# A hybrid decoder layer on one core: the first super-block loaded once, transposed, its sums of squares taken as fp32 products with a tile of ones

## The chip, the cores and the metric

The kernel runs on one core of a Trainium2 chip. The core has five engines with a queue of instructions each: TensorE (PE in the profile, its weight loads PEld), VectorE (DVE), ScalarE (ACT), GpSimd (POOL) and SyncE (SP), which here only starts transfers (DMA). Each queue runs in its own order; an instruction waits for what it needs from other queues, and everything behind it on its queue waits with it. SBUF is the memory on the chip, with 128 partitions; TensorE writes its results to PSUM.

The metric is the time of one execution on the device in microseconds, as the median of several runs. Before the change three runs took 2046.22, 2046.26 and 2054.05 us.

## The reference, cut to what matters

One layer for 2048 prompt tokens and 64 sample tokens of width 1024, in fp32. Each token is normalised by the root of its mean square, then multiplied by a wide matrix whose columns feed an attention branch, a convolution branch and a spatial gating branch; these are gated, projected and added to the input.

```python
def _rmsnorm(x, w):
    xf = x.astype(jnp.float32)
    r = lax.rsqrt(jnp.mean(xf * xf, axis=-1, keepdims=True) + EPS)
    return (xf * r).astype(x.dtype) * w
...
    xn = _rmsnorm(x, p["norm_w"])
    h = jnp.einsum("btd,de->bte", xn, p["w_in"])
    q, k, v, z_a, gate_b, gate_c, h_b, z_b, u, v_c, z_c, g = _split_cols(h)
...
    m = gates[:, :, 0] * a + gates[:, :, 1] * b + gates[:, :, 2] * c
    return x + jnp.einsum("btd,de->bte", m, p["w_o"])
```

The change concerns only how the first 512 tokens get their normalised `xn`.

## The kernel before

The tokens are worked off in four super-blocks: three of 512 prompt tokens and a last one of 512 prompt and 64 sample tokens. Within a super-block come the phases in turn: keys and values (`kv_phase`), queries (`q_phase`, a product over all token tiles that the profile calls wideS, widepv and ps_mm at lines 312 to 314, and this text the wide product), attention between the products of the convolution and chunk phases, the gates, and the output projection.

Products are made in three passes of a reduced format (fp32r): each fp32 operand is split into a high part (`split`, a copy by ScalarE, line 169) and a low part (a subtraction by VectorE, line 170), and TensorE adds high times high, high times low and low times high. So the normalised input is stored as `xh` and `xl`, with the 1024 features in 8 k tiles of 128 partitions and the tokens along the free dimension. Weights arrive as `raw` (line 119) in 512 KB pieces, three buffers ahead, and are split into `wh` and `wl`.

Later super-blocks are normalised while TensorE works on the one before (`xrstd`, `xsplit`). The first one has nothing ahead of it: `first_block` handles it in four tiles of 128 tokens. Each tile is loaded twice: `xnat` with tokens in the partitions, for the sum of squares (ScalarE's square with its accumulator, line 265), and `xin` transposed, with features in the partitions. `rstd` makes the reciprocal root on GpSimd in two instructions (lines 165 and 166). A transpose on TensorE (line 268) spreads the 128 values over all partitions, ScalarE copies them to `xrbuf` (line 271), and then, for each of the 8 k tiles, VectorE scales `xin` by the norm weight and that value (line 273) and `split` stores the two parts.

Piece 0 of `first_block` is issued before `kv_phase`. Pieces 1 to 3 are issued from inside it: `later(0.25, ...)` queues piece i + 1 so that it runs at the first `tick` of tile i, which `natural` makes after its fourth k tile. The 24 products of a tile (lines 287 to 289, 256 columns each) are thus cut in two by what piece i + 1 puts on TensorE.

TensorE's and SyncE's queues run in the order in which the code issues. The order on ScalarE, VectorE and GpSimd is set by the framework's scheduler when the kernel is built.

Of the kernel before, what the change touches and what calls it, by code (L numbers as in the profile page):

```python
# [10 lines left out]
F32 = mybir.dt.float32  # L11
F32R = mybir.dt.float32r
AF = mybir.ActivationFunctionType
ALU = mybir.AluOpType
AX = mybir.AxisListType

P = 128
D = 1024
# [6 lines left out]
KT = D // P  # L25
SLOPES = [2.0 ** -(h + 1) for h in range(8)]
TMAX = 576
# [21 lines left out]
def trunk_kernel(ctx: ExitStack, tc: tile.TileContext, A, O):  # L49
    nc = tc.nc  # L50
    consts = ctx.enter_context(tc.tile_pool(name="consts", bufs=1))
    res = ctx.enter_context(tc.tile_pool(name="res", bufs=1))
# [9 lines left out]
    def ps_tp():  # L62
        return psum.tile([P, 512], F32, tag="tp", name="ps_tp", bufs=2)
# [51 lines left out]
    def load_to(j):  # L115
        while len(loaded) < min(j, len(units)):
            src = units[len(loaded)][2]
            raw = raws.tile([P, WE], F32, tag="raw", name="raw")
            nc.sync.dma_start(raw[:, : src.shape[1]], src)
            loaded.append(raw)  # L120

    def split_to(j):
        while len(ready) < min(j, len(units)):
            i = len(ready)
            load_to(i + 1)
            n = units[i][2].shape[1]
            wh = wts.tile([P, WE], F32R, tag="wh", name="wh")
            wl = wts.tile([P, WE], F32R, tag="wl", name="wl")
            split(wh[:, :n], wl[:, :n], loaded[i][:, :n])
            loaded[i] = None  # L130
            ready.append((wh, wl))
            load_to(i + 1 + ahead["loads"])
# [11 lines left out]
    def const(name):  # L144
        src = A[name]
        t = consts.tile(list(src.shape), F32, name="c_" + name)
        nc.sync.dma_start(t, src)
        return t

    mhalf = consts.tile([P, 8], F32, name="mhalf")  # L150
    nc.gpsimd.memset(mhalf, -0.5)


    xh = res.tile([P, KT, TMAX], F32R, name="xh")
    xl = res.tile([P, KT, TMAX], F32R, name="xl")
# [1 line left out]
    vst = res.tile([P, 5 * 256 + 128], F32R, name="vst")  # L157
    hist = consts.tile([P, 4, 2], F32, name="hist")

    consts.tile([P, 48], F32, name="pad")  # L160
    nc.vector.memset(hist, 0.0)

    def rstd(out, ssq, n, width):

        nc.gpsimd.tensor_scalar(out, ssq, 1.0 / width, EPS, ALU.mult, ALU.add)
        nc.gpsimd.tensor_tensor(out, out, mhalf[: out.shape[0], :n], ALU.pow)  # L166

    def split(hi, lo, src):
        nc.scalar.copy(hi, src)  # L169
        nc.vector.tensor_tensor(lo, src, hi.bitcast(F32), ALU.subtract)  # L170
# [78 lines left out]
    def first_block():  # L249

        xin = res.tile([P, 8 * TMAX], F32, tag="mh", name="xin")
        xnat = res.tile([P, 8 * TMAX], F32, tag="ml", name="xnat")
        r = small.tile([P, 8], F32, tag="xr", name="xr")
        rbuf = res.tile([P, 4 * TMAX], F32, tag="za", name="xrbuf")
        view = lambda t, i: t[:, i * D:(i + 1) * D].rearrange("p (k t) -> p k t", k=KT)

        def load(i, natural):
            if natural:
                nc.sync.dma_start(xnat[:, i * D:(i + 1) * D], A["xn"][i * P:(i + 1) * P])
            else:  # L260
                nc.sync.dma_start(view(xin, i), A["xt"][:, :, i * P:(i + 1) * P].rearrange("k p t -> p k t"))

        def piece(i):
            sq, x = xnat[:, i * D:(i + 1) * D], view(xin, i)
            nc.scalar.activation(sq, sq, AF.Square, accum_out=r[:, i:i + 1])
            rstd(r[:, i:i + 1], r[:, i:i + 1], 1, D)
            ps = ps_tp()
            nc.tensor.transpose(ps[:, 0:P], r[:, i:i + 1].broadcast_to([P, P]), ident)
            ts = slice(i * P, (i + 1) * P)
            rb = rbuf[:, ts]  # L270
            nc.scalar.copy(rb, ps[:, 0:P])
            for k in range(KT):
                nc.vector.scalar_tensor_tensor(x[:, k], x[:, k], nw[:, k:k + 1], rb, ALU.mult, ALU.mult)
                split(xh[:, k, ts], xl[:, k, ts], x[:, k])
            if i == 3:
                ahead.update(loads=RAWS, splits=AHEAD)

        return load, piece
# [477 lines left out]
    def out_phase(sb, m):  # L756
# [12 lines left out]
        flush()  # L769

    load, prepare = first_block()
    load(0, True)
    nw = const("nw")
    ident = const("ident")
    load_to(1)
    load(0, False)
    load_to(2)
    split_to(1)
    prepare(0)
    split_to(2)  # L780
    for i in range(1, 4):
        load(i, True)
        load(i, False)
    load_to(2 + RAWS)
    knw2 = const("knw2")
    qnw2 = const("qnw2")
# [174 lines left out]
```

## Time and profile before

| | us |
|---|---|
| median of the three runs | 2046.26 |
| the profiled execution | 2048.72 |
| its span, first to last instruction | 2047.0 |
| TensorE busy in it | 2016.7 (99%) |
| VectorE busy | 1050.9 (51%) |
| ScalarE busy | 845.8 (41%) |
| GpSimd busy | 83.5 (4%) |

The busy shares are means over the whole span. A shift in the first super-block's preparation shows in the first of the page's 40 slices only (0.6 of it busy on TensorE, 0.9 or more in all others), so the views to use are those of the first 40 us: which engine waits for which, and the instructions in order of time. A row of the timeline has the start in us, the duration in us, engine, line, operation, tile written and tiles read, shape, count, and in brackets the engine's idle time before it with what ended it. A row of a group has, behind the bar, the busy time in us and the mean duration in ns, and then the idle time before.

### The profile page before, as it was taken

How to read it: one execution, taken by the hardware profiler on the slowest of the kernel's cores; microseconds unless marked ns; L12 is line 12 of the kernel's file. 1: busy time of each engine (PE TensorE's matmuls, PEld its weight loads, DVE VectorE, ACT ScalarE, POOL GpSimd, SP SyncE). 2: the span in 40 equal slices, each digit the busy share in tenths (PEclk: the TensorE clock that was granted, in tenths of full speed). 3: DMA queues.
4: the chain of work that ended last, by engine and by line, in shares of the span. 5: the costliest groups of instructions: out<-in, count | busy, mean ns of one | idle time of the engine just before them, and what ended most of it. 6: DMA issues, size and time to landing. Idle time of an engine off the chain costs nothing.

```text
span 2047.0 us, 27359 instructions
## 1 busy us (share of the span) xinstructions
PE 2016.7 (99%) x10887; PEld 1757.1 (86%) x10887; DVE 1050.9 (51%) x1818; ACT 845.8 (41%) x1462; POOL 83.5 (4%) x134
## 2 busy tenths in 40 slices
PE   6999999999999999999999999999999999999999
PEld 5788888888888888888888888888879999999999
DVE  5686263445588353335478535335537842533332
ACT  4675233332476333333267433333247641322320
POOL 2200000000200000000200000000110000000000
PEclk9999999999999999999999999999999998999999
DMA  6222233336222223336322223334522332222233
GB/s 206 82 83 83 84 101 123 114 119 210 84 82 83 88 78 126 111 93 201 119 83 81 84 82 109 118 108 136 173 83 59 64 114 57 65 85 86 78 104 108
DMA packets 85695, 212.25 MB, mean 104 GB/s; under 512 B 18224, under 2 KB 23344, under 8 KB 85552
## 3 DMA queue, kind: packets, MB, share of 16 engines
q1 hardware_dynamic: 85536, 209.53, 33.2%
q8 instruction: 85, 1.39, 0.3%
q10 hardware_dynamic: 32, 0.98, 0.1%
q14 instruction: 42, 0.34, 0.1%
HBM read 201.46 MB, written 10.00 MB: 103 GB/s over the span
## 4 chain that ended last, share of the span: by engine, by line
PE 93%; DVE 3%; ACT 2%; POOL 1%; issue 0%; DMA 0%; SPq 0%; ACTq 0%; DVEq 0%; POOLq 0%
PE ps_mm L179 26%; PE ps_mm L178 26%; PE ps_mm L180 26%; PE ps_tp L488 1%; PE wideS L313 1%; PE wideS L314 1%; PE wideS L312 1%; POOL qr L166 1%; PE ps_mm L312 1%; PE ps_mm L314 1%; PE ps_mm L313 1%; PE sp L464 1%; PE ps_mm L289 1%; PE ps_mm L287 1%; PE ps_mm L288 1%; PE pv L496 1%
## 5 line engine op out<-in xcount | busy, mean ns | idle before, releaser
L178 PE MATMUL ps_mm<-xh,wh 128*128 128x512 f32 (+1 forms) x2080 | 743.3, 357 | 5.0 <-DVE qn L409 4.5
L180 PE MATMUL ps_mm<-xh,wl 128*128 128x512 f32 (+1 forms) x2080 | 734.4, 353 | 0.0
L179 PE MATMUL ps_mm<-xl,wh 128*128 128x512 f32 (+1 forms) x2080 | 734.3, 353 | 0.0
L170 DVE TENSOR_TENSOR wl<-raw,wh 128x1024 fp32r<-128x1024 f32 x376 | 408.0, 1085 | 576.5 <-ACT wh L169 573.8
L169 ACT CAST wh<-raw 128x1024 fp32r<-128x1024 f32 x376 | 353.5, 941 | 772.1 <-PE ps_mm L179 535.4
L178 PEld LDWEIGHTS ps_mm<-xh,wh 128*128 128x128 f32 x2080 | 393.2, 189 | 51.9 <-issue 4.7
L180 PEld LDWEIGHTS ps_mm<-xh,wl 128*128 128x128 f32 x2080 | 392.6, 189 | 49.6
L179 PEld LDWEIGHTS ps_mm<-xl,wh 128*128 128x128 f32 x2080 | 393.4, 189 | 45.7
L179 PE MATMUL ps_mm<-ml,wh 128*128 128x512 f32 (+1 forms) x320 | 112.5, 351 | 0.3 <-DVE ml L170 0.3
L180 PE MATMUL ps_mm<-mh,wl 128*128 128x512 f32 (+1 forms) x320 | 112.4, 351 | 0.0
L178 PE MATMUL ps_mm<-mh,wh 128*128 128x512 f32 (+1 forms) x320 | 112.4, 351 | 0.0
L744 DVE TENSOR_TENSOR t<-ps_mm,t 128x512 f32<-128x512 f32 (+1 forms) x120 | 71.6, 597 | 73.7 <-PE ps_mm L180 73.7
L728 ACT ACTIVATE t<-ps_mm,c_bg 128x512 f32<-128x512 f32 (+1 forms) x120 | 73.0, 609 | 69.5 <-PE ps_mm L180 69.5
L450 ACT ACTIVATE rbuf<-ps_tp,c_qnw 64x256 fp32r<-64x256 f32 x128 | 60.0, 468 | 39.4 <-DVE rbuf L451 33.4
L179 PEld LDWEIGHTS ps_mm<-ml,wh 128*128 128x128 f32 x320 | 60.0, 188 | 8.0 <-DVE ml L170 0.6
L180 PEld LDWEIGHTS ps_mm<-mh,wl 128*128 128x128 f32 x320 | 60.1, 188 | 7.5
L178 PEld LDWEIGHTS ps_mm<-mh,wh 128*128 128x128 f32 x320 | 60.1, 188 | 7.4
L474 ACT ACTIVATE sbuf<-sbuf,nm 128x256 f32<-128x256 f32 (+1 forms) x128 | 62.8, 492 | 7.1 <-DVE nm L471 6.8
L767 DVE TENSOR_TENSOR xt<-ps_mm,xt 128x512 f32<-128x512 f32 (+1 forms) x40 | 23.9, 597 | 75.1 <-PE ps_mm L180 46.2
L179 PE MATMUL ps_mm<-br2l,wh 128*128 128x512 f32 (+1 forms) x160 | 56.5, 353 | 0.4 <-DVE br2l L170 0.2
L180 PE MATMUL ps_mm<-br2h,wl 128*128 128x512 f32 (+1 forms) x160 | 56.3, 352 | 0.0
L179 PE MATMUL ps_mm<-br1l,wh 128*128 128x512 f32 (+1 forms) x160 | 56.2, 352 | 0.0
(212 smaller groups left out, 2703.3 us busy)
## 6 DMA issues: line engine op xcount, KB each, us to landing
raw<-in_wt SPq DMA_DIRECT2D x208, 512.0 KB
raw<-in_wout SPq DMA_DIRECT2D x96, 256.0 KB
raw<-in_wn SPq DMA_DIRECT2D x40, 512.0 KB
raw<-in_wo SPq DMA_DIRECT2D x32, 512.0 KB
xbuf<-in_xn SPq DMA_DIRECT2D x12, 512.0 KB
xt<-in_xt SPq DMA_DIRECT2D x24, 256.0 KB
out_yt<-xt SPq DMA_DIRECT2D x24, 256.0 KB
xbuf<-in_xt SPq DMA_DIRECT2D x16, 256.0 KB
```

The costliest lines, as they stand in the source:

```text
L169: nc.scalar.copy(hi, src)
L170: nc.vector.tensor_tensor(lo, src, hi.bitcast(F32), ALU.subtract)
L178: nc.tensor.matmul(o, wh[:, ws], rh(k, c0, c1), start=k == 0, stop=False)
L179: nc.tensor.matmul(o, wh[:, ws], rl(k, c0, c1), start=False, stop=False)
L180: nc.tensor.matmul(o, wl[:, ws], rh(k, c0, c1), start=False, stop=k == kts - 1)
L312: nc.tensor.matmul(o, xh[:, k, ts], wh[:, ws], start=k == 0, stop=False)
L313: nc.tensor.matmul(o, xh[:, k, ts], wl[:, ws], start=False, stop=False)
L314: nc.tensor.matmul(o, xl[:, k, ts], wh[:, ws], start=False, stop=k == KT - 1)
L450: nc.scalar.activation(hh[half, :, e], src, AF.Copy, scale=qnw2[es])
L474: nc.scalar.activation(s[:, h, k0:], s[:, h, k0:], AF.Exp, bias=nm[:, h:h + 1], accum_out=den[:, h:h + 1])
L728: nc.scalar.activation(t[:, c0:c1], pg[:, : c1 - c0], AF.Sigmoid, bias=bg[:, 8 * b + d:8 * b + d + 1])
L744: nc.vector.tensor_tensor(t[:, c0:c1], pa[:, : c1 - c0], t[:, c0:c1], ALU.mult)
```

## The change

In the first super-block, `xnat` and its four loads are gone. ScalarE squares the transposed tile `xin` into `sqs`, without its accumulator. TensorE adds the squares over the features: eight fp32 products per token tile, the squared k tile as the weights and two columns of ones as the moving operand, into two columns of a PSUM tile. VectorE copies one of the columns to `r`, GpSimd makes the reciprocal root as before, and the transpose goes to the same PSUM tile. The scaling stays one instruction per k tile; the split is made for four k tiles in one instruction on each of the two engines, 128x512 elements where it was 128x128. The loads are issued in another order: the transposed tile 0 first, tile 1 between the first two weight pieces, then tiles 2 and 3.

```diff
+    ones = consts.tile([P, 2], F32, name="ones")
+    nc.gpsimd.memset(ones, 1.0)
...
-    consts.tile([P, 48], F32, name="pad")
+    consts.tile([P, 40], F32, name="pad")
...
-        xnat = res.tile([P, 8 * TMAX], F32, tag="ml", name="xnat")
+        sqs = res.tile([P, 8 * TMAX], F32, tag="ml", name="sqs")
...
-        def load(i, natural):
-            if natural:
-                nc.sync.dma_start(xnat[:, i * D:(i + 1) * D], A["xn"][i * P:(i + 1) * P])
-            else:
-                nc.sync.dma_start(view(xin, i), A["xt"][:, :, i * P:(i + 1) * P].rearrange("k p t -> p k t"))
+        def load(i):
+            nc.sync.dma_start(view(xin, i), A["xt"][:, :, i * P:(i + 1) * P].rearrange("k p t -> p k t"))
 
         def piece(i):
-            sq, x = xnat[:, i * D:(i + 1) * D], view(xin, i)
-            nc.scalar.activation(sq, sq, AF.Square, accum_out=r[:, i:i + 1])
+            x, sq = view(xin, i), view(sqs, i)
+            nc.scalar.activation(sqs[:, i * D:(i + 1) * D], xin[:, i * D:(i + 1) * D], AF.Square)
+
+            ps = ps_tp()
+            for k in range(KT):
+                nc.tensor.matmul(ps[:, P:P + 2], sq[:, k], ones, start=k == 0, stop=k == KT - 1)
+            nc.vector.tensor_copy(r[:, i:i + 1], ps[:, P:P + 1])
             rstd(r[:, i:i + 1], r[:, i:i + 1], 1, D)
-            ps = ps_tp()
             nc.tensor.transpose(ps[:, 0:P], r[:, i:i + 1].broadcast_to([P, P]), ident)
...
-            for k in range(KT):
-                nc.vector.scalar_tensor_tensor(x[:, k], x[:, k], nw[:, k:k + 1], rb, ALU.mult, ALU.mult)
-                split(xh[:, k, ts], xl[:, k, ts], x[:, k])
+            for k0 in range(0, KT, 4):
+                ks = slice(k0, k0 + 4)
+                for k in range(k0, k0 + 4):
+                    nc.vector.scalar_tensor_tensor(x[:, k], x[:, k], nw[:, k:k + 1], rb, ALU.mult, ALU.mult)
+                split(xh[:, ks, ts], xl[:, ks, ts], x[:, ks])
...
-    load(0, True)
+    load(0)
...
-    load(0, False)
+    load(1)
...
-    for i in range(1, 4):
-        load(i, True)
-        load(i, False)
+    load(2)
+    load(3)
```

How the queues change is read from the order of the built kernels; a row is a line, an operation, the tile written, the tiles read and the shape, and in brackets what it waits for. The order after the first super-block's keys and values is the same on every engine.

On TensorE, before, around the first tile's fourth k tile (lines 287 to 289 are its three products, line 268 the transpose of the second tile's values):

```order
L287 MATMUL ps_mm<-wh,xh 128x256 [waits Activation_49]
L288 MATMUL ps_mm<-wl,xh 128x256
L289 MATMUL ps_mm<-wh,xl 128x256 [waits DVE_49]
L268 MATMUL ps_tp<-c_ident,xr 128x128 [waits Pool_49]
L287 MATMUL ps_mm<-wh,xh 128x256 [waits Activation_49]
L288 MATMUL ps_mm<-wl,xh 128x256 [waits DVE_49]
```

The same place now (the products are lines 292 to 294, the ones' products line 268, the transpose line 271):

```order
L292 MATMUL ps_mm<-wh,xh 128x256
L293 MATMUL ps_mm<-wl,xh 128x256
L294 MATMUL ps_mm<-wh,xl 128x256
L268 MATMUL ps_tp<-ones,sqs 128x2 x8
L271 MATMUL ps_tp<-c_ident,xr 128x128 [waits DVE_49,Pool_49]
L292 MATMUL ps_mm<-wh,xh 128x256 [waits Activation_49]
```

Eight products stand ahead of the transpose, and the transpose waits for GpSimd and VectorE, which need these products' sum.

On VectorE, before, from the second weight split (line 170 with `wl`) into the second tile's scalings (line 273) and subtractions (line 170 with `xl`):

```order
L170 TENSOR_TENSOR wl<-raw,wh 128x1024 [waits DMAHW5_49]
L170 TENSOR_TENSOR xl<-xin,xh 128x128 [waits Activation_49]
L273 SCALAR_TENSOR_TENSOR xin<-xin,c_nw,xrbuf 128x128 [waits DMAHW7_49,Activation_49]
L273 SCALAR_TENSOR_TENSOR xin<-xin,c_nw,xrbuf 128x128 x2
L170 TENSOR_TENSOR xl<-xin,xh 128x128 [waits Activation_49] x2
```

VectorE now, from the copy of the first tile's sum (line 269) into the second tile (the subtraction is line 172, the scaling line 278):

```order
L269 COPY xr<-ps_tp 128x1 [waits PE_49]
L172 TENSOR_TENSOR wl<-raw,wh 128x1024 [waits DMAHW3_49,Activation_49]
L278 SCALAR_TENSOR_TENSOR xin<-xin,c_nw,xrbuf 128x128 [waits DMAHW1_49,DMAHW0_49,Activation_49]
L278 SCALAR_TENSOR_TENSOR xin<-xin,c_nw,xrbuf 128x128 x7
L172 TENSOR_TENSOR xl<-xin,xh 128x4x128 [waits Activation_49]
L172 TENSOR_TENSOR wl<-raw,wh 128x1024 [waits DMAHW5_49]
L172 TENSOR_TENSOR xl<-xin,xh 128x4x128 [waits Activation_49]
L269 COPY xr<-ps_tp 128x1 [waits PE_49]
L278 SCALAR_TENSOR_TENSOR xin<-xin,c_nw,xrbuf 128x128 [waits DMAHW4_49,Activation_49]
L278 SCALAR_TENSOR_TENSOR xin<-xin,c_nw,xrbuf 128x128 x6
L172 TENSOR_TENSOR xl<-xin,xh 128x4x128 [waits Activation_49]
L278 SCALAR_TENSOR_TENSOR xin<-xin,c_nw,xrbuf 128x128
```

Where scalings and subtractions alternated, seven or eight scalings now stand in a row, with one subtraction for four of them; the copy of a tile's sum stands behind the second subtraction of the tile before it.

On ScalarE, the first rows before (line 265 the square, 271 the copy of the transposed values) and now (264 and 274):

```order
L265 ACTIVATE xnat,xr<-xnat 128x1024 [waits DMAHW0_49]
L169 CAST wh<-raw 128x1024 [waits DMAHW3_49]
L271 COPY xrbuf<-ps_tp 128x128 [waits PE_49]
L169 CAST xh<-xin 128x128 [waits DMAHW4_49,DVE_49]
L169 CAST xh<-xin 128x128 [waits DVE_49]
```

```order
L264 ACTIVATE sqs<-xin 128x1024 [waits DMAHW0_49]
L171 CAST wh<-raw 128x1024 [waits DMAHW3_49]
L264 ACTIVATE sqs<-xin 128x1024 [waits DMAHW4_49]
L274 COPY xrbuf<-ps_tp 128x128 [waits PE_49]
L171 CAST wh<-raw 128x1024 [waits DMAHW5_49]
L171 CAST xh<-xin 128x4x128 [waits DVE_49]
```

The square of the second tile now stands between the first weight cast and the first copy, and waits for that tile's load.

## The prediction

> **What bounds the kernel now.** I looked at the windows of the engines first, cut at 35.01 us, then at TensorE's waits up to 36 us, then at the timeline around that cut. Columns of the windows: stretch, length, then busy time and count of PE, PEld, DVE, ACT, POOL, the granted clock, DMA share, GB/s.
>
> ```profile
> 0.00:35.01 35.01, 18.93 (x105) 16.44 (x105) 21.49 (x79) 20.68 (x59) 9.02 (x22) 1.00 0.65 217
> 35.01:2047.00 2011.99, 1997.77 (x10782) 1740.68 (x10782) 1029.45 (x1740) 825.11 (x1403) 74.45 (x112) 0.99 0.33 102
> ...
> PE ps_tp L268 <- POOL xr L166: 8.2, 2, 6.3
> PE ps_mm L287 <- ACT xh L169: 5.7, 5, 4.3
> PE wideS L313 <- DVE wl L170: 1.3, 1, 1.3
> PE ps_mm L289 <- DVE xl L170: 0.9, 2, 0.7
> ...
> 33.74 1.22 DVE L170 TENSOR_TENSOR wl<-raw,wh 128x1024 fp32r<-128x1024 f32 x1
> 35.01 0.50 PE L313 MATMUL wideS<-wl,xh 128*128 128x512 f32 x1 [1.26 <-DVE wl L170]
> ```
>
> From 35.01 us on TensorE is busy 1997.77 of 2011.99 us: that stretch is TensorE's own work and the edit leaves it alone. Before 35.01 it stands still for 16.1 us (35.01 - 18.93), in the four waits listed (8.2 + 5.7 + 1.3 + 0.9). The last of them ends with the weight split at 33.74. So the question is one only: **when does the unbroken wide product begin in the changed kernel, instead of at 35.01 us?** Every microsecond there goes to the end one for one.
>
> **The change, part by part.** The sums of squares leave ScalarE's accumulator for TensorE: per 128-token tile, a square without accumulation, eight fp32 products with the ones, a one-column copy by VectorE, then POOL's two operations, the transpose, ScalarE's copy and the scaling. On TensorE's queue the products and the transpose of tile i+1 stand between the fourth and fifth k tile of tile i. So in every tile TensorE itself now runs the start of a chain whose end it waits for, with all its later products queued behind that transpose. Before, the squares of tiles 2 and 3 were done early, so only two transposes waited.
>
> The chain's links, from rows of before:
>
> ```profile
> 4.23 1.06 ACT L265 ACTIVATE xnat<-xnat 128x1024 f32<-128x1024 f32 x1 [2.15 <-DMA xnat<-in_xn]
> 5.19 0.19 ACT L265 ACTIVATION_READ_ACCUMULATOR xnat<-xnat 128x1 f32 x1
> 5.46 0.19 POOL L165 TENSOR_SCALAR xr<-xr 128x1 f32<-128x1 f32 x1 [4.33 <-ACT xnat L265]
> 6.35 0.47 PE L268 MATMUL ps_tp<-c_ident,xr 128*128 128x128 f32 x1 [6.35 <-POOL xr L166]
> ...
> 16.10 0.48 PE L268 MATMUL ps_tp<-c_ident,xr 128*128 128x128 f32 x1 [1.88 <-POOL xr L166]
> 16.91 0.88 DVE L273 SCALAR_TENSOR_TENSOR xin<-xin,c_nw,xrbuf 128x128 f32<-128x128 f32 x3 [1.56 <-ACT xrbuf L271]
> 18.58 1.13 DVE L273 SCALAR_TENSOR_TENSOR xin<-xin,c_nw,xrbuf 128x128 f32<-128x128 f32 x4
> ...
> L273 DVE SCALAR_TENSOR_TENSOR xin<-xin,c_nw,xrbuf 128x128 f32<-128x128 f32 x32 | 9.5, 345 | 2.5 <-ACT xrbuf L271 2.5
> L170 DVE TENSOR_TENSOR xl<-xbuf,xh 128x512 fp32r<-128x512 f32 x16 | 10.8, 686 | 2.7 <-ACT xh L169 2.7
> L170 DVE TENSOR_TENSOR xl<-xin,xh 128x128 fp32r<-128x128 f32 x32 | 7.5, 284 | 0.0
> 19.63 1.09 DVE L170 TENSOR_TENSOR xl<-xin,xh 128x128 fp32r<-128x128 f32 x5
> L471 DVE TENSOR_TENSOR nm<-nm,nsinkb 128x4 f32<-128x4 f32 x32 | 4.9, 154 | 0.1
> ```
>
> POOL's pair, from ScalarE's end (5.19 + 0.19) to the transpose at 6.35: 0.97 us. Transpose to scaling, 16.10 to 16.91: 0.81. Scalings start every 0.26 ((1.13 - 0.345) / 3): seven take 1.86, eight 2.1. One lo subtraction of four k tiles: 0.69. The copy isn't in the trace; the nearest row is a 128x4 operation of 0.154, and with the end of the last product before it I take 0.4 (bounds 0.15 and 0.9, should a queued subtraction stand ahead).
>
> The products aren't in the trace in this shape either. Nearest are the fp32 products of the sample group:
>
> ```profile
> L671 PE MATMUL ps_tp<-wsd,vn 64*128 64x64 f32 x8 | 1.1, 278 | 0.0
> 1781.57 1.10 PE L671 MATMUL ps_tp<-wsd,vn 64*128 64x64 f32 x8
> 1668.46 0.44 PE L552 MATMUL sps<-sbuf 64*32 64x128 f32 x8
> 20.43 0.41 PE L288 MATMUL ps_mm<-wl,xh 128*128 128x256 f32 x1
> 20.64 0.41 PE L289 MATMUL ps_mm<-wh,xl 128*128 128x256 f32 x1
> 21.01 0.28 PE L288 MATMUL ps_mm<-wl,xh 128*128 128x256 f32 x1
> 21.12 0.28 PE L289 MATMUL ps_mm<-wh,xl 128*128 128x256 f32 x1
> ```
>
> Line 671 is four calls and eight records: two records for each fp32 product, one every 0.118 us ((1.10 - 0.27) / 7), with 128 weight columns as here. Eight products are then 16 records, 1.9 us; the low bound is line 552's 0.025 a record ((0.44 - 0.27) / 7, with 32 weight columns), 0.4 us a tile. I take 0.118, since the weights have the same width. The last four rows show a second thing: up to 20.64 us a 256-column product starts every 0.21 us, from 21.01 on every 0.11 to 0.12, though the granted clock reads 1.00 throughout. TensorE starts at half pace and reached the full one after working unbroken since 16.10. At half pace I double the records: 3.8 us a tile.
>
> What is removed: four loads of xn (2.1 MB), the accumulator reads, and 24 casts and 24 subtractions on ScalarE and VectorE. VectorE gains 32 x 0.20 - 8 x 0.6 - 4 x 0.15 = 1.0 us (0.20 is the start to start of the x5 row; 0.6 is 0.69 less the same 0.08 overlap). The loads hide nothing that TensorE waits for after 10 us; the first one is now in 512-byte pieces, and I take 4.7 us for it where xn was there at 4.23. A later landing moves the first step by as much, and no other.
>
> ```profile
> 14.45 0.96 POOL L165 TENSOR_SCALAR xr<-xr 128x1 f32<-128x1 f32 x1 [8.15 <-ACT xnat L265]
> 13.94 1.22 DVE L170 TENSOR_TENSOR wl<-raw,wh 128x1024 fp32r<-128x1024 f32 x1
> 22.95 0.19 POOL L165 TENSOR_SCALAR xr<-xr 128x1 f32<-128x1 f32 x1 [0.75 <-ACT xnat L265]
> ```
>
> POOL's first operation took 0.96 us at 14.45 instead of the 0.19 at 22.95, beside a weight split on VectorE. In the new order of VectorE a weight split stands right behind the copy of tile 2 and behind that of tile 0: I add 0.8 and 0.4. [...]
>
> What else VectorE has to do in a cycle, beside the weight split and the second lo half:
>
> ```profile
> L323 DVE TENSOR_REDUCE ks<-sq 128x2 f32<-128x128 f32 x4 | 1.1, 281 | 0.0
> L365 DVE TENSOR_TENSOR kd<-ps_mm,kr 128x256 f32<-128x256 f32 x3 | 1.3, 423 | 1.8 <-POOL kr L166 1.8
> L393 DVE TENSOR_TENSOR vst<-ps_mm,vst 128x128 fp32r<-128x128 f32 x3 | 0.9, 284 | 0.0
> L356 DVE SCALAR_TENSOR_TENSOR kst<-ps_tp,c_knw,kst 64x256 fp32r<-64x256 f32 x2 | 1.0, 491 | 0.0
> 10.42 0.87 DVE L273 SCALAR_TENSOR_TENSOR xin<-xin,c_nw,xrbuf 128x128 f32<-128x128 f32 x3
> ```
>
> Weight split, lo half, ks, kd and vst are 1.22 + 0.69 + 0.28 + 0.42 + 0.28 = 2.9 us; they fit beside the products and records of a cycle (1.2 + 1.9).
>
> **The sum.** Tile 0: landing 4.7, square 1.05, records 3.8, copy 0.4, POOL 0.97 + 0.4, 0.81, eight scalings 2.1, subtraction 0.69: 15.0 us. One cycle from a tile's first lo half to the next one's: ten products, 16 records, then 0.4 + 0.97 + 0.81 + 1.86 + 0.69 = 4.73. Cycle 1, half pace at first: 2.1 + 2.9 (between 1.9 and 3.8) + 4.7: 24.7. Cycle 2: 1.2 + 1.9 + 4.7 + 0.8: 33.3. Cycle 3: 7.8: 41.1. Tail: the other half of tile 3 comes 1.5 later (0.26 + 0.49 + 0.28 + 0.69, less what overlaps), its products take 1.3, two transposes and the first wide one 0.5: **44.4 us, where 35.01 was: +9.4**.
>
> The profiled execution is 2048.72 us (span 2047.0 and 1.7 around it), 2.5 above the median of the three runs; its sum becomes 2058.1. Against the median, 2046.26 + 9.4 = 2055.7.
>
> **Rivals.** *Cheap records*, 0.025 each: cycles 2 and 3 lose 1.5 each, cycle 1 2.3, tile 0 only 0.8, as ScalarE's copy then waits behind the square of tile 1 (its load has the place in the queue that tile 0's xin had, which was in use at 10.42). +3.3: 2049.6. Against it: the 128-column row. *Half pace to the end of the stage*, if small products don't raise the clock: +0.9 in cycle 1, 2.8 in each of cycles 2 and 3, 1.0 in the tail, about 2 at the start of the wide product: 9.5 more, 2065.2. For it: the pauses; against it: 4.8 us of work sufficed before. [...] *VectorE sets the pace*, and the chain hides beside its other work: only its 1.0 us of gain shows, 2045.3, no slower. It decides where products, records, copy, POOL and transpose-to-scaling (1.2 + 1.9 + 0.4 + 0.97 + 0.81 = 5.3) fall below the 2.9 us that VectorE has to do meanwhile. Even free records leave 3.4, so it is unlikely.
>
> **Chances.** Forecast (2052.5 to 2059) 0.63, cheap records 0.13, half pace 0.12, four loads 0.05, VectorE's pace 0.07. The range 2049.5 to 2065 leaves out the last and half of the half pace. A measurement can tell about 0.5% (10.2 us) from no change; 2056.5 is that bound, inside the forecast's spread: two fifths of it and the two slow rivals make 0.42 slower. Faster by 10 us would need the wide product at 25 us: 0.02. Within: 0.56.
>
> **What would show it.** Right: the wide product starts near 44 us; four transposes wait for POOL, about 1.4 us each; line 268 has 64 records about 0.12 apart once the pace is full; the lo subtractions are 8 of 0.69; after that the groups are as before. Wrong: other record counts or spacing; a half pace past 25 us; TensorE waiting for VectorE's subtraction behind a weight split rather than for POOL; or the wide product before 38 us.

## The result, and the profile after

The changed kernel took 2065.95 us (median of four runs, 2064.32 to 2068.27), the kernel before 2047.92 us (2046.22 to 2054.05): a ratio of 1.0083, with a 95% interval of 1.0058 to 1.0108. It is slower by 0.8%, 18.0 us of the medians, and the interval excludes 1. The profiled executions are 2064.32 and 2048.72 us, 15.6 apart. The forecast was +9.4, and the time lies 0.95 us above the top of its range. That range was counted from 2046.26, the median of three runs; the kernel before has 2047.92 here, 1.66 us more. The outcome that the prediction held likeliest, a change within its bound of 10.2 us (0.56), did not come; slower, at 0.42, did.

The windows of the changed kernel, cut where the second wide product begins (columns as in the prediction), and TensorE's waits up to 60 us:

```profile
0.00:49.57 49.57, 33.95 (x169) 32.05 (x170) 22.40 (x61) 17.98 (x31) 10.55 (x23) 0.83 0.43 132
49.57:2062.60 2013.03, 1998.49 (x10783) 1741.07 (x10781) 1027.35 (x1738) 825.34 (x1405) 73.74 (x113) 0.99 0.33 101
...
PE ps_tp L271 <- POOL xr L168: 6.5, 4, 2.1
PE ps_tp L268 <- ACT sqs L264: 5.9, 1, 5.9
PE ps_mm L292 <- ACT xh L171: 3.1, 2, 2.2
PE ps_mm L294 <- DVE xl L172: 0.2, 1, 0.2
```

That product starts at 49.57 instead of 35.01: 14.56 of the 15.6 us are lost ahead of it, and the other 1.0 behind it (2013.03 against 2011.99, taken up at the end). Ahead of it TensorE now stands still for 15.6 us (49.57 - 33.95) where it did for 16.1. So it waits no longer than before; it is busy for 15.0 us more. The granted clock says why that isn't 64 records alone: its mean there is 0.83.

The timeline has the cycles (start, duration, engine, line). L268 holds the products with the ones, L172 the lo half that ends a cycle:

```profile
14.43 0.68 DVE L172 TENSOR_TENSOR xl<-xin,xh 128x512 fp32r<-128x512 f32 x1
17.46 3.41 PE L268 MATMUL ps_tp<-ones,sqs 128*128 128x2 f32 x16
24.69 0.68 DVE L172 TENSOR_TENSOR xl<-xin,xh 128x512 fp32r<-128x512 f32 x1
26.95 1.84 PE L268 MATMUL ps_tp<-ones,sqs 128*128 128x2 f32 x16
34.74 0.69 DVE L172 TENSOR_TENSOR xl<-xin,xh 128x512 fp32r<-128x512 f32 x1 [1.07 <-ACT xh L171]
37.79 3.41 PE L268 MATMUL ps_tp<-ones,sqs 128*128 128x2 f32 x16
45.01 0.68 DVE L172 TENSOR_TENSOR xl<-xin,xh 128x512 fp32r<-128x512 f32 x1
49.57 0.39 PE L318 MATMUL wideS<-wl,xh 128*128 128x512 f32 x1
```

The lo halves end at 15.11, 25.37, 35.43 and 45.69. The 16 records take 1.84 us in tile 2, but 3.41 in tiles 1 and 3: in tile 3 TensorE was back at half pace. Windows of 3.41 us show when. The length is that of the shortest low stretch of the granted clock in the trace of before; the others there and in this trace last 6.83, 10.24 and 17.07 us, two, three and five times as long. The windows are cut so that the changes of the granted clock, 29.36 and 46.43 us, fall on their edges. First all work, then, in the rows behind the "...", the products with the ones alone (PE, PEld, then clock, DMA share, GB/s):

```profile
19.12:22.53 3.41, 2.24 (x12) 2.16 (x12) 0.16 (x1) 0.00 (x0) 0.74 (x2) 1.00 0.79 213
22.53:25.95 3.42, 3.42 (x16) 3.19 (x16) 3.10 (x11) 2.67 (x5) 0.03 (x1) 1.00 0.02 5
25.95:29.36 3.41, 2.85 (x26) 2.76 (x24) 2.57 (x5) 1.16 (x3) 2.37 (x3) 1.00 0.37 112
29.36:32.77 3.41, 1.91 (x9) 1.91 (x10) 2.14 (x8) 0.27 (x1) 1.36 (x2) 0.50 0.58 166
32.77:36.19 3.42, 2.55 (x11) 2.03 (x10) 2.06 (x8) 1.24 (x3) 0.19 (x1) 0.50 0.09 35
36.19:39.60 3.41, 3.41 (x19) 3.41 (x18) 1.22 (x3) 0.42 (x2) 0.70 (x1) 0.50 0.00 0
39.60:43.01 3.41, 2.25 (x11) 2.17 (x12) 0.16 (x1) 0.14 (x1) 0.73 (x2) 0.50 0.01 2
43.01:46.43 3.42, 3.42 (x18) 3.42 (x17) 2.86 (x10) 1.32 (x5) 0.00 (x0) 0.50 0.00 0
...
19.12:22.53 3.41, 1.75 (x9) 1.66 (x8) 1.00 0.79 213
25.95:29.36 3.41, 1.84 (x16) 1.88 (x16) 1.00 0.37 112
36.19:39.60 3.41, 1.81 (x10) 2.02 (x10) 0.50 0.00 0
39.60:43.01 3.41, 1.60 (x8) 1.51 (x8) 0.50 0.01 2
```

The full pace lasted for one window, 25.95 to 29.36. In it TensorE was busy for 2.85 of 3.41 us, and still the clock fell behind it, for five windows. (In the first two rows the column reads 1.00 although the products start every 0.21 us, as it does before up to 20.64 us: ahead of the first fall the spacing of the products, 0.21 us there and 0.11 to 0.12 from 25.95 on, tells the pace, and the column doesn't.)

### The profile page after: what moved, and what is told of

Its sections match the earlier page's. It is cut to its first block, busy times and chain, and to the rows that moved or that the text cites. A ratio compares the mean times of both kernels' runs of the same rounds, so it can differ in the third digit from the quotient of the medians.

```text
span 2062.6 us, 27433 instructions
## 1 busy us (share of the span) xinstructions
PE 2032.4 (99%) x10951; PEld 1773.1 (86%) x10951; DVE 1049.8 (51%) x1798; ACT 843.3 (41%) x1434; POOL 84.3 (4%) x135
## 3 DMA queue, kind: packets, MB, share of 16 engines
q8 instruction: 86, 1.41, 0.3%
## 4 chain that ended last, share of the span: by engine, by line
PE 94%; DVE 3%; POOL 2%; ACT 1%; issue 1%; DMA 0%; ACTq 0%; DVEq 0%; POOLq 0%
PE ps_mm L181 26%; PE ps_mm L180 26%; PE ps_mm L182 25%; PE ps_tp L493 1%; PE wideS L319 1%; PE wideS L318 1%; PE wideS L317 1%; POOL qr L168 1%; PE ps_mm L294 1%; PE ps_mm L292 1%; PE ps_mm L293 1%; PE ps_mm L317 1%; PE ps_mm L319 1%; PE ps_mm L318 1%; PE sp L469 1%; PE sp L468 1%
## 5 line engine op out<-in xcount | busy, mean ns | idle before, releaser
L172 DVE TENSOR_TENSOR wl<-raw,wh 128x1024 fp32r<-128x1024 f32 x376 | 408.1, 1086 | 570.1 <-ACT wh L171 567.5
```

## The experiments

Two questions: what made the clock fall, and which part of the 14.56 us is the clock's, which that of the waits on TensorE's queue. **Theory A**: products of two columns don't keep the clock up, however long TensorE is busy with them. **Theory B**: the pauses ahead of the four transposes let it fall. "Wide start" is where the second wide product begins (35.01 before, 49.57 after), in one profiled execution each.

| kernel | median us | ratio to before, 95% | wide start |
|---|---|---|---|
| grouped split alone | 2048.65 | 1.0006 [0.9996, 1.0015] | 35.40 |
| sums alone | 2060.4 | 1.0063 [1.0048, 1.0079] | 49.15 |
| 256 columns of ones | 2064.26 | 1.0083 [1.0060, 1.0105] | 50.22 |
| 128 columns | 2056.9 | 1.0040 [1.0025, 1.0055] | 45.12 |
| sums one tile ahead | 2056.33 | 1.0040 [1.0027, 1.0053] | 44.39 |
| ahead, 128 columns | 2053.27 | 1.0026 [1.0015, 1.0037] | 38.60 |
| fp32r sums | 2055.96 | 1.0039 [1.0026, 1.0052] | 41.74 |
| ahead, fp32r, 256 columns | 2051.78 | 1.0017 [1.0008, 1.0026] | 39.37 |

**The split by itself, and the sums by themselves.** The kernel before with the new split, and the changed one with the old split:

```diff
-            for k in range(KT):
-                nc.vector.scalar_tensor_tensor(x[:, k], x[:, k], nw[:, k:k + 1], rb, ALU.mult, ALU.mult)
-                split(xh[:, k, ts], xl[:, k, ts], x[:, k])
+            for k0 in range(0, KT, 4):
+                ks = slice(k0, k0 + 4)
+                for k in range(k0, k0 + 4):
+                    nc.vector.scalar_tensor_tensor(x[:, k], x[:, k], nw[:, k:k + 1], rb, ALU.mult, ALU.mult)
+                split(xh[:, ks, ts], xl[:, ks, ts], x[:, ks])
```

> The kernel before with one part of the change: the split is made four k tiles at a time; loads and sums of squares stay as before. If the sums cause the loss: the wide product starts at 34 to 37 us (35.0 before), the time within 2 us of before. If the grouped split holds back TensorE's first products of each tile: the wide product at 38 us or later, 3 us or more above before.

> The changed kernel with the split one k tile at a time, as before; the single loads and the products with ones stay. If the sums cause the loss: the wide product at 47 to 51 us, the time within 3 us of the changed kernel's. If the grouped split has a large share: 3 us or more below the changed kernel.

The split alone moves the wide start by 0.39 us and the time by nothing that can be measured; the sums alone start it at 49.15. So the later start is that of the sums (with the loads that go with them). Their time is 12.9 us above the kernel before, not 18.0; it misses the 3 us of the expectation, by which the split would have a large share. The two profiled executions don't bear that out: of their 4.06 us (2064.32 - 2060.26), 0.42 come from the wide start and 3.68 from behind it (2009.35 us against 2013.03), which the last section takes up.

**Wider products.** The changed kernel, with the ones repeated over 256 columns, and over 128 (all columns hold the same sum):

```diff
-                nc.tensor.matmul(ps[:, P:P + 2], sq[:, k], ones, start=k == 0, stop=k == KT - 1)
+                nc.tensor.matmul(ps[:, P:P + 256], sq[:, k], ones[:, 0:1].broadcast_to([P, 256]), start=k == 0, stop=k == KT - 1)
```

> As the changed kernel, but each product's moving operand is the column of ones read 256 times in place of two columns; the sums are the same and the number of records too. Theory A (two-column products do not count as work for TensorE's clock, so the clock stays or falls back to half): the clock goes full by about 22 us and stays full to the end of the stage, the wide product starts at 43 to 45 us in place of 49.6, and the time is 4 to 6 us below the changed kernel's. Theory B (the pauses in which TensorE waits for GpSimd take the clock down): the clock falls at about 29 us as before, the wide product starts within 1.5 us of 49.6. If a record is paid by its columns, the records are 0.43 us apart at the half clock and tile 0 comes 3 us later under both.

> As the run with 256 columns of ones, with 128. There the clock stayed full but each record took 0.228 us in place of 0.115, about two passes over its 256 columns. If a record costs the larger of its weight load (0.115) and two passes over its columns, 128 columns cost nothing more: records 0.11 to 0.13 us apart at the full clock, 16 in about 1.9 us. Theory A (small products let the clock fall, and that is what the forecast missed): clock full from about 20 us at the latest to the end of the stage, the wide product at 43 to 46 us, 3 to 6 us below the changed kernel. Rival C (the clock costs little here, the chain sets the time): clock full, but the wide product at 47 us or later.

The timeline of tile 2's or 3's records and of the wide start, and windows; 256 columns, then 128:

```profile
29.37 3.65 PE L268 MATMUL ps_tp<-ones,sqs 128*128 128x256 f32 x16
50.22 0.39 PE L318 MATMUL wideS<-wl,xh 128*128 128x512 f32 x1
...
13.67:17.09 3.42, 0.82 (x3) 0.43 (x3) 2.56 (x9) 2.61 (x4) 0.14 (x1) 1.00 0.95 336
26.00:50.22 24.22, 19.08 (x117) 15.98 (x115) 13.33 (x42) 7.18 (x18) 5.43 (x12) 1.00 0.00 1
```

```profile
35.32 1.95 PE L268 MATMUL ps_tp<-ones,sqs 128*128 128x128 f32 x16
45.12 0.40 PE L318 MATMUL wideS<-wl,xh 128*128 128x512 f32 x1
...
20.00:45.00 25.00, 18.80 (x134) 16.70 (x134) 14.12 (x46) 7.33 (x18) 6.06 (x14) 1.00 0.16 54
```

With 128 columns the clock stays full once it has risen; with 256 it rises in tile 0 already (at 10.26 by the spacing), falls once at 17.09, behind the first window above with TensorE busy for 0.82 us in it, and is full again from 20.50. From there on it reads 1.00 to the end of the stage in both, and the products lie 0.12 us apart, though TensorE is busy for only 79% and 75% of these windows. With 256 columns the wide start is no earlier, which the expectation missed: the records now lie 0.225 us apart ((3.65 - 0.28) / 15) and cost what the clock saves. With 128 they lie 0.112 apart ((1.95 - 0.27) / 15), as with two columns (0.111 at full clock, 1.84 - 0.17 over 15), and 4.45 us are gained (49.57 - 45.12). A product of 256 columns is two records of 0.225 us here, each twice the 0.11 to 0.12 between the 256-column fp32r products in the prediction; from 2 to 128 columns the record costs no more. That the weight load sets this floor is an estimate from the prediction's rows (0.118 with 128 weight columns, 0.025 with 32); no run tried it alone.

**The sums one tile ahead.** The products of tile i + 1 are issued ahead of tile i's transpose, into a PSUM tile of their own, so that three of the four transposes find their sums done:

```diff
+        sums = psum.tile([P, 512], F32, tag="S0", name="sums", bufs=1)
+        def squares(i):
...
+                nc.tensor.matmul(sums[:, 2 * i:2 * i + 2], sq[:, k], ones, start=k == 0, stop=k == KT - 1)
...
         def piece(i):
+            if 0 < i < 3:
+                squares(i + 1)
             ps = ps_tp()
             nc.tensor.transpose(ps[:, 0:P], r[:, i:i + 1].broadcast_to([P, P]), ident)
+            if i == 0:
+                squares(1)
```

> The changed kernel, but the products of tile i + 1 are issued one tile earlier than its transpose, in a PSUM buffer of their own, so that copy and GpSimd's two instructions run beside other products. Both theories: TensorE's waits for GpSimd fall from 6.5 us to about 2 (the first alone). Theory A (two-column products do not count as work): the clock is still at half for most of the stage, 64 records at 0.21 us or 0.12, the wide product at 42 to 46 us. Theory B (pauses take the clock down): once full, at about 20 us, it stays full, the wide product at 37 to 40 us.

TensorE's wait for POOL, then two windows:

```profile
PE ps_tp L277 <- POOL xr L168: 2.1, 1, 2.1
...
26.60:30.00 3.40, 3.09 (x27) 2.89 (x26) 2.81 (x5) 1.73 (x3) 2.12 (x2) 1.00 0.22 33
30.00:33.40 3.40, 3.40 (x17) 3.12 (x16) 2.49 (x11) 0.43 (x2) 0.73 (x2) 0.51 0.33 127
```

The three pauses are gone, and the clock falls all the same, at 30.08, behind a window with TensorE busy for 3.09 of 3.40 us. So this fall doesn't need those pauses, and theory B doesn't explain it.

**Both, and fewer records.** The order of the last kernel with 128 columns; the changed kernel with ones and squares in the reduced format, which makes one record of a product (8 in a tile); and the new order, the reduced format and 256 columns together:

```diff
-                nc.tensor.matmul(sums[:, 2 * i:2 * i + 2], sq[:, k], ones, start=k == 0, stop=k == KT - 1)
+                nc.tensor.matmul(sums[:, 128 * i:128 * i + 128], sq[:, k], ones[:, 0:1].broadcast_to([P, 128]), start=k == 0, stop=k == KT - 1)
```

```diff
-    ones = consts.tile([P, 2], F32, name="ones")
+    ones = consts.tile([P, 2], F32R, name="ones")
-        sqs = res.tile([P, 8 * TMAX], F32, tag="ml", name="sqs")
+        sqs = res.tile([P, 8 * TMAX], F32R, tag="ml", name="sqs")
```

> Products one tile ahead of the transposes, and 128 columns of ones: both the waits for GpSimd and the half clock are taken away, the 64 records stay. Cycle at the full clock: 1.2 us of products, 1.9 of records, 0.81 to the scaling, 1.86 scaling, 0.69 subtraction, 6.5 in all. Theory A: the wide product at 37 to 41 us. Rival C: clock worth little, 42 to 44 us (44.1 with two columns). In no case before 35: the chain through VectorE stays longer than before.

> The changed kernel with squares and ones in the reduced format (fp32r), two columns: the sums are taken with that precision. One record for each product in place of two: 8 in a tile, 0.9 us at the full clock, 1.7 at half. Theory A: these are small products too, so the clock is still at half for most of the stage; what is saved is 1.7 us in each cycle at half clock, the wide product at 43 to 46 us. Rival C: the same saving or less, 45 to 48 us. If fp32r weights load slower than fp32, records are more than 0.13 us apart at the full clock and nothing is saved.

> The three cures together: products one tile ahead of the transposes, squares and ones in the reduced format (one record for each product, so the sums have that precision), and 256 columns of ones, which one pass takes in about the time of a weight load, so that the clock stays full. A cycle on TensorE is 1.2 of products, 0.95 of records, 0.81 to the scaling, 1.86 scaling, 0.69 subtraction: 5.5 us, and VectorE's own work in a cycle is about 6. So the wide product at 35 to 38 us: at most 3 us above before, and not below it by more than the spread of runs. If it starts before 34 us, the single load and the grouped split have a gain that the sums had hidden.

Width and order add up. In the changed kernel's order, two columns start the wide product at 49.57, 128 columns at 45.12; ahead, it is 44.39 and 38.60. So the width is worth 4.45 to 5.79 us, the order 5.18 to 6.52. The fp32r kernel came out at 41.74, better than expected, with one low window. The last one started at 39.37, later than expected. Its clock fell, too, 256 columns notwithstanding, behind this window:

```profile
20.09:23.51 3.42, 1.41 (x10) 1.00 (x8) 2.65 (x10) 1.73 (x3) 0.69 (x2) 1.00 0.84 245
```

TensorE had been busy for 1.41 of 3.42 us, with no two-column product in it. The same holds for the fall with 256 columns above, and for one of the kernel ahead with 128 columns (low from 16.16 to 19.58, behind 1.12 us). So in these windows pauses count by themselves, and narrow products count like pauses (1.01 us is left of the 2.85 when they are taken out); theory A was too narrow.

**A count, and two kernels to try it.** One more execution of the changed kernel, of 2062.11 us, showed that the fall repeats:

> The changed kernel once more, for the clock alone. If the fall of the clock in the first 50 us comes from the two-column products and not from the place of one execution in the clock's windows, it is at half again for 10 us or more between 20 and 47 us, and the wide product starts at 47 to 51 us. If it was the luck of one execution: full from about 25 us, the wide product at 43 to 46 us.

```profile
30.00:36.00 6.00, 3.85 (x16) 3.33 (x16) 3.66 (x13) 1.05 (x3) 1.14 (x2) 0.52 0.32 95
36.00:42.00 6.00, 5.62 (x26) 5.53 (x26) 1.70 (x6) 0.88 (x2) 0.99 (x3) 0.50 0.00 0
50.00 0.40 PE L318 MATMUL wideS<-wl,xh 128*128 128x512 f32 x1
```

**Theory C** takes all windows together: count TensorE's busy time in each window less that in two-column products. In the changed kernel that is 2.85 - 1.84 = 1.01 us ahead of the fall, then 1.91, 2.55, 1.60 and 0.65 with no rise, and 3.42 ahead of the rise at 46.43. It also explains the late first rise: 0.49 from 19.12 to 22.53, then 3.42. (The two expectations below rest on windows that begin 0.36 us sooner, hence other counts in them, 1.38 ahead of the fall.) To try it, 128 columns for one tile only, tile 2 in one kernel and tile 3 in the other:

```diff
+                w = 128 if i == 2 else 2
-                nc.tensor.matmul(ps[:, P:P + 2], sq[:, k], ones, start=k == 0, stop=k == KT - 1)
+                nc.tensor.matmul(ps[:, P:P + w], sq[:, k], ones[:, 0:1].broadcast_to([P, w]), start=k == 0, stop=k == KT - 1)
```

> The changed kernel, with 128 columns of ones in place of 2 for the products of tile 2 alone. Theory C, read from the windows of the earlier runs: the clock is set anew every 3.41 us by what TensorE did in the last 3.41 us; time in two-column products counts as idle; it falls when about 1.6 us or less of a window counts, and rises only when over 2.6 us of one does. By it the clock holds through tile 2 (the window that counted 1.38 counts over 3) and falls first behind tile 3's two-column products, near 36 us. The second wide product begins at 45.5 to 47.5, between the 45.12 with 128 columns in all tiles and the 49.57 of the change. Rival: the clock falls for a reason that has nothing to do with the width of the products (the order of pauses, a chance of the phase); then it falls near 29 as in both executions of the change, and the wide product begins at 49 to 50.

> The changed kernel, with 128 columns of ones for the products of tile 3 alone. Theory C: the clock falls near 29 as before, since tile 2's products are unchanged; the next two windows count 1.5 and 2.5 us and leave it low; the third, which held 3.41 us of TensorE time of which 1.45 were two-column products, now counts whole, so the clock rises near 39 us and not at 46. The second wide product begins at 47 to 49. Rival (width doesn't matter): the clock stays at half until 46 and the wide product begins at 49 to 50.

They took 2056.44 and 2062.96 us in one run each, with 2044.57 for the kernel before beside them. Windows of the first kernel, then the same for the products with the ones alone, and the wide start:

```profile
28.10:31.50 3.40, 1.66 (x13) 1.54 (x13) 1.78 (x8) 0.27 (x1) 0.74 (x2) 1.00 0.60 195
34.90:38.30 3.40, 2.24 (x20) 2.15 (x20) 1.32 (x5) 0.53 (x2) 0.74 (x2) 1.00 0.01 2
38.30:41.70 3.40, 3.40 (x16) 3.07 (x15) 3.34 (x12) 1.87 (x4) 0.00 (x0) 0.50 0.00 0
...
34.90:38.30 3.40, 1.40 (x13) 1.31 (x12) 1.00 0.01 2
...
44.32 0.40 PE L319 MATMUL wideS<-wl,xh 128*128 128x512 f32 x1
```

And of the second:

```profile
27.65:31.05 3.40, 2.08 (x19) 2.00 (x18) 1.93 (x5) 0.27 (x1) 1.82 (x2) 1.00 0.43 154
31.05:34.45 3.40, 2.65 (x13) 2.66 (x13) 2.13 (x10) 0.27 (x1) 0.61 (x2) 0.51 0.53 154
37.85:41.25 3.40, 2.24 (x20) 2.05 (x19) 1.38 (x4) 0.40 (x2) 0.74 (x2) 1.00 0.01 2
...
27.65:31.05 3.40, 1.84 (x16) 1.87 (x16) 1.00 0.43 154
37.85:41.25 3.40, 1.75 (x16) 1.56 (x14) 1.00 0.01 2
...
47.44 0.39 PE L319 MATMUL wideS<-wl,xh 128*128 128x512 f32 x1
```

With tile 2 wide, the clock held through it and fell behind tile 3's narrow products, as C says; this low stretch was one window only, and the wide start of 44.32 is below the 45.5 to 47.5 expected. There was another, from 21.21 to 24.62, behind tile 1's narrow products (0.48 counted). The expectation didn't have it, since here the clock had risen at 17.79 already, and in the changed kernel's profile at 25.95: how the windows lie differs between these executions. With tile 3 wide, the fall came behind tile 2's narrow products (2.08 - 1.84 = 0.24 counted), at 31.1, and tile 3's wide ones held the clock; the rise came two windows sooner than expected, since the windows lay otherwise and the next one counted 2.65. The pair to look at is 34.90 to 38.30 of the first and 37.85 to 41.25 of the second: TensorE is busy for 2.24 of 3.40 us in both. In the first 1.40 of it are two-column products and the clock falls; in the second 1.75 are 128-column products and it holds.

## Where the prediction was right, and where it was wrong

Right were these steps:
- The wide start sets the time, and what follows is as before but for 1.0 us.
- Tile 0 ends at 15.11 (15.0 was forecast, though its terms add up to 14.9) and cycle 1 at 25.37 (24.7). The load landed at 4.67 (4.7).
- Four transposes wait for POOL, 6.5 us in all, 1.6 each (1.4). The records are 64, 0.111 us apart at the full clock (0.118). The lo subtractions are 8 of 0.68.
- POOL's first operation, beside a weight split, takes 1.11 and 1.09 us (0.96 was the row it rested on):

```profile
9.71 1.11 POOL L167 TENSOR_SCALAR xr<-xr 128x1 f32<-128x1 f32 x1 [8.54 <-DVE xr L269]
21.16 0.19 POOL L167 TENSOR_SCALAR xr<-xr 128x1 f32<-128x1 f32 x1 [9.70 <-DVE xr L269]
29.08 1.09 POOL L167 TENSOR_SCALAR xr<-xr 128x1 f32<-128x1 f32 x1 [0.95 <-DVE xr L269]
```

**The step that failed** is the pace of cycles 2 and 3: 8.6 and 7.8 us were summed at the full clock; they took 10.06 and 10.26, and the tail 3.9 instead of 3.3. With 0.7 from tile 0 and cycle 1 that is 5.2 us, the difference between the forecast's +9.4 and the +14.56. In cycle 3 the half pace acts directly: its first ten products take 2.36 us (35.43 to 37.79) for the 1.2 of the sum, its records 3.41 for 1.9. In cycle 2 the records are at the full pace (1.84), and the larger part of the loss is a wait that the sum doesn't have:

```profile
33.93 0.28 ACT L326 ACTIVATE sq<-ps_mm 128x128 f32<-128x128 f32 x1 [2.29 <-PE ps_mm L294]
34.10 0.61 ACT L171 CAST xh<-xin 128x512 fp32r<-128x512 f32 x1
```

On ScalarE's queue the square of tile 1's keys stands ahead of the cast of tile 2's first half. It waits for tile 1's last 12 products, which TensorE makes at half pace from 30.99 on; VectorE's lo subtraction then waits 1.07 us for the cast (the row at 34.74 above). At 0.12 us in place of 0.21 these products would have ended about 1.1 us sooner, an estimate. So this loss, too, is the clock's, by way of another queue. With 128 columns for tile 2 the cast stands ahead of the square (31.67 and 32.20 in the kernel with tile 2 alone wide), so a part of what the width gains may be this order; the two were not tried apart.

What was against the half pace in the prediction, that 4.8 us of unbroken work had sufficed before, held for 256-column products; the new cycle has the work (2.85 of 3.41 us), but 1.84 us of it in two-column products, and the clock fell behind it.

So the rival called half pace to the end of the stage is the one that came, with one window of full clock in it, and with it the prediction's sign of being wrong, a half pace past 25 us. Its time, 2065.2, is near the median, but not for its reasons alone: it put 9.5 us more into the stage and the start of the wide product, where 5.2 came. The rest of the 10.3 us between the sum, 2055.7, and the median is luck: 1.0 behind the wide start, 1.7 by which the kernel before came out above the median that the sum started from, and 2.4 by which medians and profiled executions differ (18.0 and 15.6). Four loads to a product, at 0.05 in the chances and in their sum for slower, is out: no run shows four, and the records are 16 a tile, two for each product. Cheap records is out, too: 0.111 us with 128 weight columns, not 0.025. VectorE never set the pace.

Of the 14.56 us, 4.5 to 5.8 go with the width of the products, and so mostly with the clock, and 5.2 to 6.5 with the transposes that TensorE waits for with all else behind them. The two aren't cleanly apart: with the sums ahead the low stretch lasts one window instead of five. The last 3.6 (38.60 - 35.01) are left when both are cured: TensorE then waits less than before (12.8 us in all, against 16.1) and is busy 6.8 us longer. Its 64 records take 10.3 us there, some at half pace, and all its other work 3.5 us less than before (15.4 against 18.9). That is the sum of one execution; no kernel without the records was tried in that order. None of the variants beats the kernel before; the split alone is level with it.

## What to carry to other kernels

A product that is moved to an engine that has idle time isn't free there if the engine then waits for its own result in order (6.5 us here): issue such sums a step ahead of their use, which moved the wide start from 49.57 to 44.39. When products are priced, two prices count, the floor of a record (0.11 us here, with 2 columns as with 128) and the clock: here a window with TensorE busy for 2.85 of 3.41 us, 1.84 of it in two-column products, was followed by five at a clock of 0.50. Check the granted clock in windows cut where it changes (3.41 us long here), ahead of trusting durations from another stage.

## What was not expected of the hardware

**What the clock counts.** In the changed kernel the fall and the rise are 17.07 us apart, five windows of 3.41. In ten of the thirteen profiled executions the clock falls ahead of the wide product, twelve times in all, and each low stretch is one, two or five such windows. Cut at these edges and counted as in theory C, it fell behind windows of 0.20 to 1.57 us (1.01 and 1.41 above; 1.57 is the sums one tile ahead, whose rows above are cut 0.07 us off and count 1.63) and held behind 1.54 (256 columns, 10.26 to 13.67), 1.61 and more. It rose behind 2.72 and 2.73 in two cases and behind 2.88 and more in all, and not behind 2.64 and less; nor did it behind two windows of 2.79 and 2.84 before the first rise. These counts are what the thirteen profiles show, read after the runs; they are sharp to 0.1 us or so, an estimate from the 0.06 us by which a cut 0.07 us off moves one. That two-column products don't count was tried by itself, in the pair of windows with 2.24 us above; the counts at which the clock turns were not.

**Low windows later in the run.** The clock falls again far behind the change, and in the kernel before as well. There it falls at 1700.2 us, for three windows, behind this one (all work, then the products of lines 593 and 594 alone, of 32 columns each, tile yps):

```profile
1696.80:1700.21 3.41, 3.41 (x31) 2.81 (x30) 0.00 (x0) 0.41 (x1) 0.00 (x0) 1.00 0.53 154
1696.80:1700.21 3.41, 3.37 (x30) 2.81 (x30) 0.00 (x0) 1.00 0.53 154
```

TensorE is busy throughout, with narrow products. So the trace of before had a sign of what the prediction missed, though not in the first super-block.

How much differs between executions: 13.7 us of low clock in all in two of the profiles, 17.1, 20.5 and 23.9 in others, each a number of whole windows. The time behind the wide start follows it, by some 0.36 us for each us ((2013.03 - 2009.35) / 10.2): sums alone and sums ahead (13.7), then the changed kernel (23.9):

```profile
49.15:2058.50 2009.35, 1995.12 (x10783) 1738.06 (x10781) 1027.42 (x1737) 825.42 (x1406) 73.47 (x113) 1.00 0.33 101
```

```profile
44.39:2053.40 2009.01, 1994.78 (x10783) 1737.96 (x10781) 1028.75 (x1739) 826.01 (x1406) 74.39 (x113) 1.00 0.33 101
```

The kernel before had 20.5 us and took 2011.99. The one window more, 3.4 us at 0.36, is 1.2 us by that slope, about the 1.0 us that the changed kernel lost behind the wide start. All thirteen profiles, of whatever kernel, keep this order: behind the wide start they take 2009.0 to 2009.4 us with 13.7 us of low clock, 2010.2 to 2011.1 with 17.1, 2011.8 to 2012.3 with 20.5 and 2013.0 to 2013.8 with 23.9. So up to 4.8 us between two executions have nothing to do with the change, the 3.68 us of the sums alone among them. What sets the number in an execution stays open.
